# The first stage of a hybrid encoder step: weights in halves, squares behind the high halves, additions on VectorE

## The chip, the cores and the metric

The kernel runs on one core of one Trainium2 chip. Its time is device microseconds of one execution; the time of a kernel is the median of several executions. A core has five engines that work through their own queues in order and wait for one another by semaphores: TensorE (PE: matrix products; its weight loads are listed apart as PEld), VectorE (DVE), ScalarE (ACT), GpSimd (POOL) and SyncE (SP, which here issues DMAs). PE multiplies out of SBUF into PSUM, of which this kernel uses eight banks of 128 x 512 float32.

## The reference

One layer of an encoder runs over 1024 prompt rows and 128 decode rows (8 requests of 16), 1152 rows of 1024 features:

```python
h = rmsnorm(x, p['g_pre1'])
z = h @ p['w_in']                       # 1024 columns: SSM 512, pooling 256, memory queries 256
y_ssm, ... = s5_scan(u_ssm, ...)        # diagonal state space
y_pool, pool_new = multiscale_pool(u_pool, ...)
y_mem = memory_attention(q_mem, mk, mv) # mk, mv: rmsnorm(mem) @ w_mem_k, w_mem_v
gates = jax.nn.sigmoid(h @ p['w_gate'] + p['b_gate'])
merged = sum over branches of gates * (y @ w_br)
x = x + rmsnorm(merged @ p['w_out'], p['g_post1'])
x = x + rmsnorm(conv_ffn(rmsnorm(x, p['g_pre2'])), p['g_post2'])
```

with `rmsnorm(x, g) = x * rsqrt(mean(x*x) + 1e-6) * g`. Only the first normalisation, the first columns of `z`, and the normalisation and products of the 256 memory tokens are touched here.

## The kernel before, in words

Activations lie transposed: features on the 128 partitions in 8 slices (k), the rows in three chunks of 384 columns. Each float32 operand of a product is split in two: a high part, rounded to TensorE's fast format, and a low part, the rest. For a weight, `split` has ACT write `whi` (L63) and DVE `wlo` (L64). For the activations, `feat_split` has ACT write `hhi` (L126, times the gain) and DVE `hlo` (L127), slice by slice. `mm3` then makes three products for each slice (L103 hhi by whi, L106 hlo by whi, L107 hhi by wlo), so a tile of 128 output columns by one chunk (`z_tile`) is 24 products of 128x384.

The factor rsqrt(mean) is not applied before the product. While PE multiplies the unscaled rows, the sums of squares are made beside it: `feat_sq` squares a chunk in four pieces of two slices (L140 on ACT, or L142 on POOL), adds them in pairs (L144, on POOL), and adds the two rests on DVE (L148, L149). `feat_cols` has PE sum over the partitions (L156, three small products, one for each block of 128 rows, into the bank `ss`). `rsqrt` is ACT's `rs_v` (L84) and POOL's power -0.5, `rs_y` (L86). `row_bcast` has ACT write three diagonal matrices (L94 `diag`), which PE multiplies by ones (L96), so that the factor of each row stands in all partitions; ACT copies it to `rb` (L177). Then `done` scales the finished tile (`scaled`, DVE L200, `sg`) and sends it to DRAM in pieces (L883).

`start` does this for the first three blocks of `w_in` (two, called the pair, and the third, `w2`) over the three chunks, and then makes the memory tokens' keys and values (`mem_load`, `mem_split`, `mem_kv`, `mem_out`). The finished tiles lie in PSUM until `rb` of their chunk is there. PSUM has two tags of four banks: "c" (`pc`) and "s" (`ps`); a fifth `pc` tile waits until `done` has read the first one. The SSM's parameters (`ssm_params`, L343 to L441, many small DVE instructions on `pr` tiles) and the first tables (L460 to L508) are put between by a scheduler.

The order on each engine comes from that scheduler: it takes instructions by priority as written, as soon as it holds them to be ready. `keep_in_program_order` (the `pin` arguments) keeps PE's products in the order of the code, `issue_after(i)` puts what follows behind instruction i on i's own engine, `high_priority` pulls ahead. Buffers: `raw` (weights as loaded) three, `w1` (split weights) six, that is three pairs; the four square tiles share the tags U (two buffers), CA and V; `sg` three.

Before the change the order in `start` is: PE makes tile 0 and 1 of chunk 0, half of tile 0 of chunk 1, then sums chunk 0's squares, then the rest of chunk 1, and so on; ACT squares chunk 0 between its high halves.

Of the kernel before, what the change touches and what calls it, by code (L numbers as in the profile page):

```python
# [32 lines left out]
class K:  # L33
# [100 lines left out]
    def feat_sq(self, P, x, n, tags, engs="AAAA", add=True):  # L134
        nc = self.nc
        sq = [P.tile([128, 2, n * 128], F32, tag=t, name="sq") for t in tags]
        for a in range(4):
            xa = x[:, 2 * a:2 * a + 2]
            if engs[a] == "A":
                nc.scalar.activation(sq[a], xa, AF.Square)  # L140
            else:
                (nc.vector if engs[a] == "V" else nc.gpsimd).tensor_mul(sq[a], xa, xa)  # L142
            if a % 2:
                nc.gpsimd.tensor_add(sq[a - 1], sq[a - 1], sq[a])  # L144
        parts = [sq[i][:, k] for i in (0, 2) for k in range(2)]
        if add:
            with self.tc.high_priority():
                nc.vector.tensor_add(sq[0], sq[0], sq[2])  # L148
                nc.vector.tensor_add(parts[0], parts[0], parts[1])  # L149
# [112 lines left out]
    def start(self, P, pair, done, z):  # L262
# [34 lines left out]
        self.h_tiles()  # L297
        self.h_split(x2, lo)
        self.h_rows(P, rms(0, 3), 0, True)
        with self.tc.issue_after(self.diag.ins):  # L300
            self.h_split(x2, up)
# [13 lines left out]
        with self.tc.issue_after(self.diag.ins):
            w2 = self.load_w(I["w_in"][2])
            q2 = self.feat_sq(P, x2, 3, tags, "AAAA")
# [9 lines left out]
            xm = self.mem_load()  # L327
            wk = [self.load_w(I["w_mk"][h], sh) for h in range(2)]
            self.feat_sums(P, xm, 2, ss[:, 9:11], tags, "AAAA")
            mem = self.mem_split(xm)  # L330
            rsm = self.mem_rows(P, rms(9, 2))
            self.mem_out(P, "mk", self.mem_kv(mem, "mk", wk), *rsm)
# [1511 lines left out]
```

## Time and profile before

| | us |
|---|---|
| median of the runs (3) | 1606.23 |
| lowest, highest | 1605.18, 1611.32 |
| the profiled execution | 1607.13 |
| its span | 1605.3 |
| PE busy in the span | 1546.5 (96%) |
| weight loads busy | 1512.9 (94%) |
| DVE busy | 1044.1 (65%) |
| ACT busy | 586.4 (37%) |
| POOL busy | 510.8 (32%) |

A profile is one execution. Each of its rows has a source line, an engine, an operation, and the tiles as "out<-in"; L126 is line 126 of the kernel before. An engine is busy when it computes, not when it waits or issues DMAs. The time behind "idle" is how long the engine stood before an instruction, and the name behind the arrow is what ended that: the instruction that came last of those it waited for. A wait matters to the end only where PE stands still for it, since PE is busy nearly all the time. A busy PE can still be slow: the granted clock says which share of its full clock TensorE had.

### The profile page before, as it was taken

Reading aid. Unit: us, or ns where it says so; the run is one execution under the profiler, and the core shown is the slowest. Engines: PE = TensorE matmul, PEld = TensorE weight load, DVE = VectorE, ACT = ScalarE, POOL = GpSimd, SP = SyncE. Lnnn points to the kernel's source line nnn. Section 1 sums busy time; section 2 is a strip of 40 time slices with the busy share of each in tenths; the row PEclk is TensorE's granted clock in tenths of the full one; section 3 lists DMA queues with packets and bytes.
Section 4 is the critical chain, followed back from the end, with each engine's and each line's share of the span. In section 5 each row is a group of like instructions: output and inputs, shape, how many; then the busy total and the mean of one; then the engine's idle time right before and its main releaser. Section 6 shows DMA issues by size and latency. Waiting matters only on the chain.

```text
span 1605.3 us, 22914 instructions
## 1 busy us (share of the span) xinstructions
PE 1546.5 (96%) x8964; PEld 1512.9 (94%) x8964; DVE 1044.1 (65%) x1602; ACT 586.4 (37%) x894; POOL 510.8 (32%) x460
## 2 busy tenths in 40 slices
PE   6899999999999999999889999999999999999996
PEld 5899999789899999999879999999999998999996
DVE  7873997655743354637777565656565658788866
ACT  6322544442421242435435433333333333333321
POOL 2400001100021143300016435443443326655546
PEclk9899999999999999999789999999999999999998
DMA  6343333434332235122323211221212143133214
GB/s 247 98 150 96 101 110 107 162 106 117 105 120 81 67 84 164 54 91 91 114 89 138 82 69 66 72 82 69 76 62 82 70 136 137 48 101 105 89 65 167
DMA packets 98460, 163.44 MB, mean 102 GB/s; under 512 B 23216, under 2 KB 68656, under 8 KB 98352
## 3 DMA queue, kind: packets, MB, share of 16 engines
q1 hardware_dynamic: 97920, 161.75, 30.5%
q8 instruction: 70, 1.15, 0.3%
q14 instruction: 38, 0.31, 0.1%
q10 hardware_dynamic: 432, 0.23, 0.0%
HBM read 119.52 MB, written 42.42 MB: 101 GB/s over the span
## 4 chain that ended last, share of the span: by engine, by line
PE 80%; DVE 9%; DMA 3%; issue 2%; ACT 2%; POOL 1%; POOLq 0%; SPq 0%; DVEq 0%; ACTq 0%
PE pc L107 15%; PE pc L103 15%; PE pc L106 14%; PE ps L103 11%; PE ps L106 11%; PE ps L107 11%; DMA Ts<-DG 1%; PE ps L849 1%; DMA DG<-gs 1%; DVE wlo L64 1%; DVE Xs L598 1%; PE ps L1072 1%; DVE mg L1124 1%; PE ps L763 0%; DVE sg L200 0%
## 5 line engine op out<-in xcount | busy, mean ns | idle before, releaser
L103 PE MATMUL pc<-hhi,whi 128*128 128x384 f32 x760 | 259.1, 341 | 7.3 <-ACT hhi L126 7.3
L106 PE MATMUL pc<-hlo,whi 128*128 128x384 f32 x760 | 258.4, 340 | 2.7 <-DVE hlo L127 2.7
L107 PE MATMUL pc<-hhi,wlo 128*128 128x384 f32 x760 | 257.9, 340 | 0.3 <-DVE wlo L64 0.3
L63 ACT ACTIVATE whi<-rawt 128x1024 fp32r<-128x1024 f32 x102 | 107.5, 1055 | 188.6 <-PE pc L106 83.4
L64 DVE TENSOR_TENSOR wlo<-rawt,whi 128x1024 fp32r<-128x1024 f32 x102 | 128.5, 1262 | 56.2 <-ACT whi L63 55.8
L103 PEld LDWEIGHTS pc<-hhi,whi 128*128 128x128 f32 x760 | 144.6, 190 | 9.8 <-ACT hhi L126 7.3
L106 PEld LDWEIGHTS pc<-hlo,whi 128*128 128x128 f32 x760 | 144.2, 190 | 5.4 <-DVE hlo L127 3.6
L107 PEld LDWEIGHTS pc<-hhi,wlo 128*128 128x128 f32 x760 | 144.3, 190 | 2.3 <-issue 0.7
L200 DVE TENSOR_TENSOR sg<-pc,rb 128x384 f32<-128x384 f32 x95 | 52.3, 553 | 117.8 <-PE pc L107 117.4
L107 PE MATMUL pc<-h2hi,wlo 128*128 128x384 f32 x352 | 119.1, 338 | 2.1 <-DVE wlo L64 2.0
L103 PE MATMUL pc<-h2hi,whi 128*128 128x384 f32 x352 | 118.3, 336 | 0.0
L106 PE MATMUL pc<-h2lo,whi 128*128 128x384 f32 x352 | 118.2, 336 | 0.0
L63 ACT ACTIVATE S<-S 128x512 fp32r<-128x512 f32 x88 | 55.3, 630 | 157.9 <-PE ps L107 89.8
L64 DVE TENSOR_TENSOR S<-S,S 128x512 fp32r<-128x512 f32 x88 | 72.5, 826 | 56.2 <-ACT S L63 54.2
L924 ACT ACTIVATE sg<-sg,vec 128x384 f32<-128x384 f32 x72 | 44.1, 613 | 139.0 <-DVE sg L200 108.3
L1011 POOL TENSOR_TENSOR mg<-mg,sgl 128x384 f32<-128x384 f32 x24 | 29.1, 1212 | 165.4 <-DVE sgl L1009 162.0
L103 PE MATMUL ps<-bT,S 128*128 128x384 f32 x240 | 80.2, 334 | 0.0
L107 PE MATMUL ps<-bT,S 128*128 128x384 f32 x240 | 80.2, 334 | 0.0
L106 PE MATMUL ps<-bT,S 128*128 128x384 f32 x240 | 80.2, 334 | 0.0
L63 ACT ACTIVATE dhi<-dwr 128x1024 fp32r<-128x1024 f32 x38 | 39.7, 1058 | 95.2 <-PE pc L106 60.7
L107 PEld LDWEIGHTS pc<-h2hi,wlo 128*128 128x128 f32 x352 | 66.1, 188 | 2.8 <-DVE wlo L64 2.8
L1244 POOL TENSOR_TENSOR S<-rawt 128x512 f32<-128x512 f32 x20 | 27.2, 1361 | 125.6 <-PE ps L107 125.6
(463 smaller groups left out, 4349.7 us busy)
## 6 DMA issues: line engine op xcount, KB each, us to landing
rawt<-in_w_up SPq DMA_DIRECT2D x48, 512.0 KB, 3.4
Dact<-t SPq DMA_DIRECT2D x22, 576.0 KB, 3.5
rawt<-in_w_gate SPq DMA_DIRECT2D x24, 512.0 KB, 3.6
dwr<-in_w_down SPq DMA_DIRECT2D x22, 512.0 KB, 3.4
Dsg<-sg SPq DMA_DIRECT2D x45, 192.0 KB, 1.9
sgl<-Dsg SPq DMA_DIRECT2D x45, 192.0 KB, 2.4
dBr<-Dact SPq DMA_DIRECT2D x8, 768.0 KB, 5.7
xT<-in_xT SPq DMA_DIRECT2D x12, 384.0 KB, 7.6
```

The lines of the kernel that those rows point to most:

```text
L63: nc.scalar.activation(hi, src, AF.Copy)
L64: (eng or nc.vector).tensor_sub(lo, src, hi)
L103: i = nc.tensor.matmul(out, whi, xhi, start=start, stop=False)
L106: nc.tensor.matmul(out, whi, xlo, start=False, stop=False)
L107: nc.tensor.matmul(out, wlo, xhi, start=False, stop=stop)
L200: self.nc.vector.tensor_mul(sg, b, self.rb[:, c, :])
L598: V.tensor_tensor(Xs[64 * i:64 * i + 64, :, g, 1:128], m1[h, :, 0:127], m2[h, :, 0:127], op=op)
L849: nc.tensor.matmul(o, va[:, m, 2 * hp + e, :], pT[:, m, :], start=m == 0, stop=m == 1)
L924: self.nc.scalar.activation(sg, sg, AF.Sigmoid, bias=self.vec[:, V_BGATE + m:V_BGATE + m + 1])
L1011: nc.gpsimd.tensor_add(m, m, sp)
L1072: m = nc.tensor.matmul(s3[:, t:t + 1], s[:, t * 128:t * 128 + 128], self.ones[:, 0:1], start=(i, t) == (0, 0), stop=(i, t) == (len(ss) - 1 ...
L1244: G.tensor_sub(s3, a11, a21)
```

## The change

All of it is in the first stage.

- The first weight block is loaded by two DMAs of four slices each and split in two halves; chunk 0's slices 0 to 3 are split between them, slices 4 to 7 behind them.
- Squares all run on ACT. Chunk 0's stand behind the high halves of chunk 1 (`issue_after(a.ins)`), chunk 1's behind those of chunk 2.
- The additions in pairs (L144) go from POOL to DVE.
- PE sums chunk 0's squares behind both whole tiles of chunk 1, and not between the halves of the first. The row broadcast of chunk 0 stands in the middle of tile 0 of chunk 2, the sums of chunk 1 behind that tile.
- The memory tokens are split like the activations, slice by slice with the gain in the instruction (ACT L126, DVE L127, `mhi`, `mlo`); before, POOL multiplied by the gain (L224) and made the low part (L64).

```diff
             if a % 2:
-                nc.gpsimd.tensor_add(sq[a - 1], sq[a - 1], sq[a])
+                nc.vector.tensor_add(sq[a - 1], sq[a - 1], sq[a])
...
     def mem_split(self, x):
-        for a in range(2):
-            ks = slice(4 * a, 4 * a + 4)
-            nc.gpsimd.tensor_mul(x[:, ks], x[:, ks],
-                                 self.vec[:, V_GMEM + 4 * a:V_GMEM + 4 * a + 4, None].to_broadcast([128, 4, 256]))
-            self.split(mhi[:, ks], mlo[:, ks], x[:, ks], nc.gpsimd)
+        self.feat_split(x, mhi, mlo, V_GMEM, range(8))
...
-        rw = [self.load_raw(I["w_in"][pair[0]])]
+        halves = slice(0, 4), slice(4, 8)
+        rw = [self.rawtile([128, 8, 128])]
+        for hs in halves:
+            nc.sync.dma_start(rw[0][:, hs], I["w_in"][pair[0]][:, hs])
...
         a, v = self.h_split(x0, (0, 1))
-        w = [self.load_w(None, r=rw[0])]
+        w = [[self.w1.tile([128, 8, 128], F32R, tag="w", name=n) for n in ("whi", "wlo")]]
+        self.split(w[0][0][:, halves[0]], w[0][1][:, halves[0]], rw[0][:, halves[0]])
         lo, up = range(4), range(4, 8)
         with self.tc.issue_after(a.ins), self.tc.issue_after(v.ins):
-            self.h_split(x0, range(2, 8))
+            self.h_split(x0, (2, 3))
+            self.split(w[0][0][:, halves[1]], w[0][1][:, halves[1]], rw[0][:, halves[1]])
+            self.h_split(x0, up)
             b0 = [self.z_tile(w[0], 0, pin=True)]
             w.append(self.load_w(None, r=rw[1]))
-            q0 = self.feat_sq(P, x0, 3, tags, "AGAA")
-        self.h_tiles()
-        self.h_split(x1)
-        b0.append(self.z_tile(w[1], 0, pin=True))
-        t = self.pc()
-        self.z_tile(w[0], 1, t, lo, True)
-        self.feat_cols(q0, 3, ss[:, 0:3], True)
-        b1 = [self.z_tile(w[0], 1, t, up, True)]
-        b1.append(self.z_tile(w[1], 1, pin=True))
...
+            self.h_tiles()
+            a, _ = self.h_split(x1)
+            b0.append(self.z_tile(w[1], 0, pin=True))
+            with self.tc.issue_after(a.ins):
+                q0 = self.feat_sq(P, x0, 3, tags)
+            b1 = [self.z_tile(w[0], 1, pin=True)]
+            self.h_tiles()
+            a, _ = self.h_split(x2)
+            b1.append(self.z_tile(w[1], 1, pin=True))
+            self.feat_cols(q0, 3, ss[:, 0:3], True)
+            with self.tc.issue_after(a.ins):
+                q1 = self.feat_sq(P, x1, 3, tags)
+            t = self.sm()
+            self.z_tile(w[0], 2, t, lo, True)
+            self.h_rows(P, rms(0, 3), 0, True)
             for i in range(2):
                 done(pair[i], 0, b0[i])
-            q1 = self.feat_sq(P, x1, 3, tags, add=True)
-            t = self.sm()
-            self.z_tile(w[0], 2, t, lo, True)
+            b2 = [self.z_tile(w[0], 2, t, up, True)]
             self.feat_cols(q1, 3, ss[:, 3:6], True)
-            b2 = [self.z_tile(w[0], 2, t, up, True)]
+            q2 = self.feat_sq(P, x2, 3, tags)
```

What a scheduler makes of it is seen in the order of the instructions. First ACT, from its first split on, before the change (`rawt` is a weight as loaded, `xT` a chunk of activations, `sq` its squares; x4 means four of them in a row):

```order
L63 ACTIVATE whi<-rawt 128x1024
L126 ACTIVATE hhi<-xT,vec 128x384 x4
L140 ACTIVATE sq<-xT 128x768
L126 ACTIVATE hhi<-xT,vec 128x384 x2
L140 ACTIVATE sq<-xT 128x768
L126 ACTIVATE hhi<-xT,vec 128x384 x2
L140 ACTIVATE sq<-xT 128x768
L63 ACTIVATE whi<-rawt 128x1024
L126 ACTIVATE hhi<-xT,vec 128x384 x12
L84 ACTIVATE rs_v<-ps 128x3
```

and the same place now:

```order
L63 ACTIVATE whi<-rawt 128x512
L126 ACTIVATE hhi<-xT,vec 128x384 x4
L63 ACTIVATE whi<-rawt 128x512
L126 ACTIVATE hhi<-xT,vec 128x384 x4
L63 ACTIVATE whi<-rawt 128x1024
L126 ACTIVATE hhi<-xT,vec 128x384 x8
L140 ACTIVATE sq<-xT 128x768 x4
L126 ACTIVATE hhi<-xT,vec 128x384 x8
L140 ACTIVATE sq<-xT 128x768
L63 ACTIVATE whi<-rawt 128x1024
```

The first weight stands in two pieces, and chunk 0's squares have moved behind the high halves of chunk 1 (the x8 ahead of them).

Next DVE from the same point on, before:

```order
L64 TENSOR_TENSOR wlo<-rawt,whi 128x1024
L127 SCALAR_TENSOR_TENSOR hlo<-xT,vec,hhi 128x384 x8
L64 TENSOR_TENSOR wlo<-rawt,whi 128x1024
L127 SCALAR_TENSOR_TENSOR hlo<-xT,vec,hhi 128x384
L148 TENSOR_TENSOR sq<-sq 128x768
L127 SCALAR_TENSOR_TENSOR hlo<-xT,vec,hhi 128x384 x4
L149 TENSOR_TENSOR sq<-sq 128x384
```

and now:

```order
L64 TENSOR_TENSOR wlo<-rawt,whi 128x512
L127 SCALAR_TENSOR_TENSOR hlo<-xT,vec,hhi 128x384 x4
L64 TENSOR_TENSOR wlo<-rawt,whi 128x512
L127 SCALAR_TENSOR_TENSOR hlo<-xT,vec,hhi 128x384 x4
L64 TENSOR_TENSOR wlo<-rawt,whi 128x1024
L127 SCALAR_TENSOR_TENSOR hlo<-xT,vec,hhi 128x384 x8
L144 TENSOR_TENSOR sq<-sq 128x768 x2
L127 SCALAR_TENSOR_TENSOR hlo<-xT,vec,hhi 128x384 x2
L148 TENSOR_TENSOR sq<-sq 128x768
L127 SCALAR_TENSOR_TENSOR hlo<-xT,vec,hhi 128x384 x3
```

The pair additions L144 stand on DVE behind the low halves of chunk 1, and the last addition L149 comes two rows further down.

Last, DVE where chunk 1's squares are added, before (`pr` with a number is a parameter of the SSM):

```order
L421 RECIPROCAL pr_909<-pr_909 128x16
L200 TENSOR_TENSOR sg<-pc,rb 128x384 x2
L363 SCALAR_TENSOR_TENSOR pr_827<-pr_827,pr_849 128x16
L381 TENSOR_SCALAR pr_874<-pr_865 128x32
L382 SCALAR_TENSOR_TENSOR pr_866<-pr_865 128x32
L148 TENSOR_TENSOR sq<-sq 128x768
L363 SCALAR_TENSOR_TENSOR pr_827<-pr_827,pr_849 128x16
L383 TENSOR_SCALAR pr_874<-pr_866 128x32
L149 TENSOR_TENSOR sq<-sq 128x384
```

and now:

```order
L64 TENSOR_TENSOR wlo<-rawt,whi 128x1024
L357 TENSOR_SCALAR pr_843<-pr_841 128x16
L144 TENSOR_TENSOR sq<-sq 128x768
L358 TENSOR_SCALAR pr_843<-pr_843 128x16
L144 TENSOR_TENSOR sq<-sq 128x768
L359 SCALAR_TENSOR_TENSOR pr_844<-pr_843,pr_841 128x16
L364 TENSOR_SCALAR pr_838<-pr_843 128x16
L148 TENSOR_TENSOR sq<-sq 128x768
L360 SCALAR_TENSOR_TENSOR pr_844<-pr_843,pr_844 128x16
L365 TENSOR_SCALAR pr_838<-pr_838 128x16
L149 TENSOR_TENSOR sq<-sq 128x384
L361 TENSOR_SCALAR pr_839<-pr_844 128x16
```

The four additions stand together ahead of most of the parameters, and `done` of chunk 0 (the two L200) comes behind them.

More of the change, by code (lines that the diff above doesn't have):

```diff
@@ L217, in mem_split @@
     def mem_split(self, x):
-        nc = self.nc
         mhi = self.mtile([128, 8, 256], F32R, "mhi")
         mlo = self.mtile([128, 8, 256], F32R, "mlo")
-        for a in range(2):
-            ks = slice(4 * a, 4 * a + 4)
-            nc.gpsimd.tensor_mul(x[:, ks], x[:, ks],
-                                 self.vec[:, V_GMEM + 4 * a:V_GMEM + 4 * a + 4, None].to_broadcast([128, 4, 256]))
-            self.split(mhi[:, ks], mlo[:, ks], x[:, ks], nc.gpsimd)
+        self.feat_split(x, mhi, mlo, V_GMEM, range(8))
         return mhi, mlo
@@ L281, in start @@
         a, v = self.h_split(x0, (0, 1))
-        w = [self.load_w(None, r=rw[0])]
+        w = [[self.w1.tile([128, 8, 128], F32R, tag="w", name=n) for n in ("whi", "wlo")]]
+        self.split(w[0][0][:, halves[0]], w[0][1][:, halves[0]], rw[0][:, halves[0]])
         lo, up = range(4), range(4, 8)
         with self.tc.issue_after(a.ins), self.tc.issue_after(v.ins):
-            self.h_split(x0, range(2, 8))
+            self.h_split(x0, (2, 3))
+            self.split(w[0][0][:, halves[1]], w[0][1][:, halves[1]], rw[0][:, halves[1]])
+            self.h_split(x0, up)
             b0 = [self.z_tile(w[0], 0, pin=True)]
             w.append(self.load_w(None, r=rw[1]))
-            q0 = self.feat_sq(P, x0, 3, tags, "AGAA")
-        self.h_tiles()
-        self.h_split(x1)
-        b0.append(self.z_tile(w[1], 0, pin=True))
-        t = self.pc()
-        self.z_tile(w[0], 1, t, lo, True)
-        self.feat_cols(q0, 3, ss[:, 0:3], True)
-        b1 = [self.z_tile(w[0], 1, t, up, True)]
-        b1.append(self.z_tile(w[1], 1, pin=True))
[L297 to L301, printed above, removed]
+            self.h_tiles()
[13 more added lines that the diff above has]
+            self.h_rows(P, rms(0, 3), 0, True)
             for i in range(2):
                 done(pair[i], 0, b0[i])
-            q1 = self.feat_sq(P, x1, 3, tags, add=True)
-            t = self.sm()
-            self.z_tile(w[0], 2, t, lo, True)
+            b2 = [self.z_tile(w[0], 2, t, up, True)]
             self.feat_cols(q1, 3, ss[:, 3:6], True)
-            b2 = [self.z_tile(w[0], 2, t, up, True)]
+            q2 = self.feat_sq(P, x2, 3, tags)
             t = self.pc()
@@ L311, in start @@
             self.h_rows(P, rms(3, 3), 1, True)
+            behind = self.tc.issue_after(self.diag.ins)
             b2.append(self.z_tile(w[1], 2, t, up, True))
@@ L314, in start @@
                 done(pair[i], 1, b1[i])
-        with self.tc.issue_after(self.diag.ins):
             w2 = self.load_w(I["w_in"][2])
-            q2 = self.feat_sq(P, x2, 3, tags, "AAAA")
             done(2, 0, self.z_tile(w2, 0, pin=True))
@@ L326, in start @@
             done(2, 2, b)
[L327 to L332, printed above, removed]
+            with behind:
+                xm = self.mem_load()
+                wk = [self.load_w(I["w_mk"][h], sh) for h in range(2)]
+                self.feat_sums(P, xm, 2, ss[:, 9:11], tags, "AAAA")
+                mem = self.mem_split(xm)
+                rsm = self.mem_rows(P, rms(9, 2))
+                self.mem_out(P, "mk", self.mem_kv(mem, "mk", wk), *rsm)
             z(3)
```

## The prediction

> **What bounds the kernel now.** I read the page first (TensorE, called PE, is busy 96% of the span), then the waits of PE, then the busy time by windows of 20 us, since a share over 1605 us hides a stage. Columns: window, its length, then busy us (and instructions) of PE, weight loads, VectorE (DVE), ScalarE (ACT) and GpSimd (POOL), the granted TensorE clock, the DMA share, GB/s.
>
> ```profile
> 0.00:20.00 20.00, 10.04 (x38) 9.14 (x39) 13.33 (x16) 15.60 (x26) 6.53 (x13) 1.00 0.93 352
> 20.00:40.00 20.00, 14.84 (x85) 14.26 (x84) 18.58 (x69) 8.99 (x20) 4.91 (x3) 0.93 0.42 144
> 40.00:60.00 20.00, 15.03 (x71) 14.44 (x72) 18.15 (x49) 9.34 (x17) 8.19 (x5) 0.84 0.36 109
> 60.00:80.00 20.00, 19.70 (x100) 19.05 (x100) 17.29 (x29) 5.51 (x11) 10.61 (x6) 0.89 0.33 87
> 80.00:100.00 20.00, 20.00 (x147) 19.95 (x146) 17.81 (x58) 8.46 (x12) 3.22 (x9) 1.00 0.60 199
> 100.00:120.00 20.00, 20.00 (x117) 20.00 (x117) 10.98 (x40) 1.54 (x2) 0.25 (x2) 1.00 0.29 104
> ```
>
> PE is the bound, and from 80 us on it has no hole. In the first 60 us it idles 20.1 us, and the granted clock is below 1 in three windows. DVE is busy 85.2 us of the first 100, so it could take PE's place there; from 100 us on it has 9 us free in 20. Where PE's holes are, its timeline says (start, length, line, operation, in brackets the idle time before and what ended it):
>
> ```profile
> 7.30 0.69 PE L103 MATMUL pc<-hhi,whi 128*128 128x384 f32 x1 [7.30 <-ACT hhi L126]
> ...
> 9.86 0.69 PE L106 MATMUL pc<-hlo,whi 128*128 128x384 f32 x1 [1.87 <-DVE hlo L127]
> ...
> 11.97 0.69 PE L106 MATMUL pc<-hlo,whi 128*128 128x384 f32 x1 [0.78 <-DVE hlo L127]
> ...
> 16.62 0.40 PE L103 MATMUL pc<-hhi,whi 128*128 128x384 f32 x1
> ...
> 23.97 0.72 PE L156 MATMUL ps<-ones,sq 128*128 128x1 f32 x6
> ...
> 24.56 0.42 PE L103 MATMUL pc<-hhi,whi 128*128 128x384 f32 x1
> ...
> 38.96 1.44 PE L156 MATMUL ps<-ones,sq 128*128 128x1 f32 x6 [5.16 <-DVE sq L149]
> 40.26 0.67 PE L103 MATMUL ps<-hhi,whi 128*128 128x384 f32 x1
> ...
> 44.16 0.33 PE L103 MATMUL pc<-hhi,whi 128*128 128x384 f32 x1
> ...
> 58.29 1.44 PE L156 MATMUL ps<-ones,sq 128*128 128x1 f32 x6 [4.97 <-DVE sq L149]
> 59.59 0.67 PE L103 MATMUL pc<-hhi,whi 128*128 128x384 f32 x1
> ...
> 64.53 0.34 PE L103 MATMUL pc<-hhi,whi 128*128 128x384 f32 x1
> ...
> 70.28 0.81 PE L96 MATMUL ps<-diag,ones 128*128 128x384 f32 x2
> ```
>
> Three places: a slow start, and twice a wait for L149, the last addition of the squares of chunks 1 and 2. Behind each wait the clock is low. Fast, a product costs 0.174 us (from 64.53 to 70.28 stand 33 of them); behind the first wait 12 cost 3.90 us (40.26 to 44.16), 0.325 each, and behind the second 15 cost 4.94 us.
>
> Why L149 is late, DVE's and POOL's rows say; the last seven are groups by form (count, busy us, mean ns).
>
> ```profile
> 6.73 1.47 POOL L142 TENSOR_TENSOR sq<-xT 128x768 f32<-128x768 f32 x1 [5.09 <-DMA xT<-in_xT]
> 6.78 2.50 DVE L64 TENSOR_TENSOR wlo<-rawt,whi 128x1024 fp32r<-128x1024 f32 x1 [5.86 <-ACT whi L63]
> 9.20 7.48 DVE L127 SCALAR_TENSOR_TENSOR hlo<-xT,vec,hhi 128x384 fp32r<-128x384 f32 x8
> ...
> 19.13 2.20 DVE L127 SCALAR_TENSOR_TENSOR hlo<-xT,vec,hhi 128x384 fp32r<-128x384 f32 x4
> 30.92 3.64 POOL L144 TENSOR_TENSOR sq<-sq 128x768 f32<-128x768 f32 x2 [4.67 <-DVE pr L363]
> 31.03 1.76 DVE L371 TENSOR_TENSOR pr<-par,pr 128x16 f32<-128x16 f32 x1
> ...
> 37.32 0.95 DVE L148 TENSOR_TENSOR sq<-sq 128x768 f32<-128x768 f32 x1
> ...
> 38.36 0.55 DVE L149 TENSOR_TENSOR sq<-sq 128x384 f32<-128x384 f32 x1
> ...
> L503 DVE TENSOR_TENSOR CA<-pr,bc 128x576 f32<-128x576 f32 x1 | 2.9, 2942 | 0.0
> L506 DVE TENSOR_TENSOR CA<-pr,bc 128x576 f32<-128x576 f32 x1 | 0.7, 744 | 0.0
> L149 DVE TENSOR_TENSOR sq<-sq 128x256 f32<-128x256 f32 x1 | 2.5, 2510 | 0.0
> L148 DVE TENSOR_TENSOR sq<-sq 128x512 f32<-128x512 f32 x1 | 2.4, 2365 | 3.8 <-POOL sq L144 3.8
> L495 DVE TENSOR_TENSOR ar<-ar,tg 128x512 f32<-128x512 f32 x1 | 0.7, 683 | 0.0
> L400 DVE TENSOR_TENSOR pr<-pr 128x64 f32<-128x64 f32 x1 | 1.9, 1878 | 0.0
> L363 DVE SCALAR_TENSOR_TENSOR pr<-pr,pr 128x16 f32<-128x16 f32 x12 | 2.0, 168 | 0.1
> ```
>
> Two POOL additions run from 30.92 to 34.56, and a DVE instruction on 16 columns that starts 0.11 us after them takes 1.76 us, where L363's of that size take 0.17. Equal shapes cost 2.94 or 0.74 (L503, L506), 2.37 or 0.68 (L148, L495); eight hlo cost 0.94 each beside POOL's first additions and 0.55 alone. So POOL's long instructions hold DVE up, and both L149 stand behind such stretches on POOL and DVE.
>
> **The change, part by part.**
>
> *Start.* For the low half wlo, DVE begins at 6.78 and takes 2.50; PE starts at 7.30, waits for the first hlo until 9.86, and again 0.78.
>
> ```profile
> 5.68 1.06 ACT L63 ACTIVATE whi<-rawt 128x1024 fp32r<-128x1024 f32 x1 [3.23 <-DMA rawt<-in_w_in]
> 13.84 6.18 ACT L126 ACTIVATE hhi<-xT,vec 128x384 fp32r<-128x384 f32 x12
> 24.98 1.27 POOL L86 TENSOR_TENSOR rs_y<-rs_v,mhalf 128x3 f32<-128x3 f32 x1 [9.79 <-ACT rs_v L84]
> 26.29 0.99 ACT L94 ACTIVATE diag<-ident,rs_y 128x128 f32<-128x128 f32 x3 [1.39 <-POOL rs_y L86]
> L140 ACT ACTIVATE sq<-mem 128x512 f32<-128x512 f32 x4 | 2.5, 622 | 3.1 <-DVE sq L148 3.1
> ```
>
> Half the weight is 256 KB less to wait for: at the 352 GB/s of the first window 0.75 us, so ACT starts near 4.95 instead of 5.68. A half costs ACT 0.62 (the 128x512 row), the first hhi 0.52 (12 in 6.18), DVE 0.68 for its half of wlo, 0.55 for the first hlo: 4.95 + 0.62 + 0.68 + 0.55, with a tenth for each hand-over, gives 7.0. Nothing runs on POOL then, so a hlo comes every 0.55 us, faster than PE's three cold products (0.98). PE runs without a hole from 7.0 instead of 9.86 with a later hole of 0.78: **3.6 us**. Bounds: 2.9 if the half lands no sooner than the whole; 4.2 if the first product, which ran ahead at 7.30, counts too. The extra DMA costs SP one issue, ahead of transfers that land behind one another anyway: nothing.
>
> *Squares behind the high halves.* ACT runs 8 hhi and the next weight before chunk 0's four squares; PE's L156 of chunk 0 moves from behind 60 products to behind 96. PE: cold for some 6 us as before (9.86 to 16.62 less the hole), 18 products until 12.9, 78 at 0.174 until 26.5. Until then ACT has halves, 8 hhi, the next whi, 8 hhi (to 15.5) and 4 squares (to 18.5); DVE, with 16 hlo at 0.55 and its weights, is through at 16.9 and then adds 2 x 0.95, 0.95, 0.55 with five hlo between: L149 ends near 23.6. PE comes 2.9 us later, so this wait stays at zero.
>
> *First stall.* L149 of chunk 1 needs four squares, of which the last needs a buffer that chunk 0's L149 frees; it stands on ACT behind rs_v, which waits for L156: done near 28.3. Two additions, L148 and L149 after it on DVE: 28.3 + 0.95 + 0.95 + 0.55 = 30.8. PE reaches it after 24 products and the row broadcast, near 32.6. The stall goes with its cold tail: 5.16 + (1.30 - 0.59 for L156) + (3.90 - 12 x 0.174) = **7.7 us**. Bound: 0 to 1 us of it stays.
>
> *Second stall.* In the same way 4.97 + 0.71 + (4.94 - 15 x 0.174) = **8.0 us**: L149 of chunk 2 ends near 36.7, PE is there near 42.4.
>
> *What is late next.* L96 of chunk 0 now stands 12 products behind L156 instead of 36. From L156's end (24.56 + 0.13) to the diagonal (27.28) are 2.6 us; 12 products are 2.1. So PE waits **0.5 us**, and 0.1 at chunk 1's. Holes that short (0.78 at 11.97) did not restart the cold stretch.
>
> Rule beside row: behind waits of 5.16 and 4.97 us the cold stretches last 5.2 us (38.96 to 44.16) and 6.2 (58.29 to 64.53). [...]
>
> *DVE's load.* New on it: six additions of 128x768 (0.95), two of 128x512 (0.68), eight mlo of 128x256 (at most 0.55): at most 11.5 us. Gone with POOL's work: wlo 2.50 - 1.37, hlo 7.48 - 4.4, L371 1.76 - 0.17, L503 2.2, L149 2.0, L148 1.7, L400 at least 1.3: 13.0 from the rows shown. DVE does not grow. What POOL keeps is rs_y; its memory tokens' product and split go to ACT (eight mhi) and DVE.
>
> *Behind the stage* the order of every engine's instructions is the old one but for a few neighbours; PE has no idle time there that a shift by some us changes.
>
> Sum: 3.6 + 7.7 + 8.0 - 0.6 = 18.7 us. The profiled execution took 1607.13 us (span 1605.3), so 1588.4; the median of the runs, 1606.23, lies 0.9 lower, which gives 1587.5. I say **1588**.
>
> **The rivals.**
> - *Banks.* The second product of w_in[2] needs a PSUM bank that done(pair, 1) frees; its row evacuation rb stands on ACT behind the next whi, three squares and eight mhi. From the diagonal at 35.5: 1.06 + 3 x 0.62 + 8 x 0.52 + 0.5 gives 43.1 with L200's 0.5 to come, where PE is at 43.2. With lower costs of mhi (a third less data than hhi) it is just in time; if not, PE waits 1 to 5 us: 1589 to 1593.
> - *No gain at the start.* If the halves bring none of the 3.6 us: 1592. [...] Against it, the row above: 384 and 512 KB pieces ran the first window at a DMA share of 0.93.
> - *DVE gets behind.* 85.2 - 13.0 + 11.5 = 83.7 us of work after a start near 5.7 ends at 89.4, where PE wants to be, at what was 100.9, at 82.2. Held back by all of it, PE loses 7.2: 1595. Against it: PE has four banks, so three tiles of 24 x 0.174 us of slack, and DVE 9 us free in the window behind.
> - *Slower: DVE becomes the bound.* If its long instructions have a cause other than POOL, nothing is relieved: 85.2 + 11.5 us, every L149 and every low weight of the first 100 us comes up to 11.5 us later than before, and PE waits there: up to 1618. It decides when a 128x16 instruction takes over 1 us with POOL idle. The pairs of equal shapes speak against it.
>
> **How the numbers follow.** Forecast 0.68 (own range 1584 to 1591, from the bounds: gain 16 to 23), banks 0.10, start 0.09, DVE behind 0.08, slower 0.05. The range of 8 in 10 reaches from 1583.5 to 1596 and leaves out the slower case and tails. Half a per cent, about what a measurement tells from no change, is 8 us: faster is below 1598.2, which takes all cases but the last and a tail of DVE behind: 0.91; same 0.04; slower 0.05.
>
> **What would show it.** In the changed profile: PE from near 7.0 with no hole over 0.3 us until L96; L156 of chunk 0 near 26.5; no wait for L149; a wait of about 0.5 us for diag; L96 of chunk 2 near 51.6 instead of 70.28; no DVE instruction of 16 columns over 1 us; clock 1.00 in every window behind the first. Wrong it would be if PE waited over 2 us for L149, L200 or whi before 60 us, or if the 18.7 us were there at 70 us and gone at 160.

## The result, and the profile after

The changed kernel took 1586.47 us (median of 4 runs, 1585.59 to 1588.48), the kernel before 1607.98 on the same chip (4 runs): a ratio of 0.9873, with a 95% interval from 0.9855 to 0.9891. The forecast of 1588, in its range of 1583.5 to 1596, held. The profiled execution took 1587.11 us with a span of 1585.3, which is 20.0 less than the span before.

One execution of one experiment (before_dve) ran at a granted clock of 0.68; it is left out of that ratio, and its rows come from a second run of the same kernel, before_dve2.

First PE's waits in the first 200 us of the changed kernel (total us, times, longest):

```profile
PE pc L103 <- ACT hhi L126: 6.6, 1, 6.6
PE ps L96 <- ACT diag L94: 1.2, 1, 1.2
PE pc L107 <- DVE wlo L64: 0.7, 2, 0.4
```

The two waits for L149 (10.1 us) and those for hlo (2.7) have gone. What is left of the first stage's waits after the start is 1.2 for the diagonal and 0.7 for low weights (0.39 at 13.81, 0.29 at 54.37). The windows of 20 us, columns as before:

```profile
0.00:20.00 20.00, 12.96 (x62) 11.74 (x63) 12.62 (x23) 15.04 (x26) 1.08 (x10) 1.00 0.93 339
20.00:40.00 20.00, 18.80 (x107) 17.63 (x107) 18.86 (x46) 18.09 (x38) 2.07 (x2) 1.00 0.58 190
40.00:60.00 20.00, 19.71 (x114) 19.05 (x114) 19.26 (x104) 8.37 (x18) 2.08 (x2) 1.00 0.51 143
```

In the first 60 us PE is busy 51.5 us where it was 39.9, the clock is 1.00 in all three, and GpSimd (POOL) has 5.2 us of work where it had 19.6. The places in PE's timeline on which the sum rested:

```profile
6.59 0.69 PE L103 MATMUL pc<-hhi,whi 128*128 128x384 f32 x1 [6.59 <-ACT hhi L126]
7.34 0.69 PE L106 MATMUL pc<-hlo,whi 128*128 128x384 f32 x1
...
10.07 0.35 PE L103 MATMUL pc<-hhi,whi 128*128 128x384 f32 x1
...
26.07 0.72 PE L156 MATMUL ps<-ones,sq 128*128 128x1 f32 x6
...
30.19 0.91 PE L96 MATMUL ps<-diag,ones 128*128 128x384 f32 x2 [1.18 <-ACT diag L94]
...
33.02 0.72 PE L156 MATMUL ps<-ones,sq 128*128 128x1 f32 x6
...
42.96 0.72 PE L156 MATMUL ps<-ones,sq 128*128 128x1 f32 x6
...
51.97 0.81 PE L96 MATMUL ps<-diag,ones 128*128 128x384 f32 x2
```

The last of these, the row scale of chunk 2, is the mark by which all kernels below are compared: it stood at 70.28, so the first stage gained 18.3 us. The rows of VectorE (DVE) that PE waited for, or could have:

```profile
23.99 0.55 DVE L149 TENSOR_TENSOR sq<-sq 128x384 f32<-128x384 f32 x1
...
30.73 0.55 DVE L149 TENSOR_TENSOR sq<-sq 128x384 f32<-128x384 f32 x1
...
36.70 0.56 DVE L149 TENSOR_TENSOR sq<-sq 128x384 f32<-128x384 f32 x1
...
39.59 0.17 DVE L371 TENSOR_TENSOR pr<-par,pr 128x16 f32<-128x16 f32 x1
...
42.66 1.01 DVE L200 TENSOR_TENSOR sg<-pc,rb 128x384 f32<-128x384 f32 x2
```

Each L149 now ends 1.5 to 5.7 us ahead of the L156 that reads it, and L371, 1.76 us before, takes 0.17.

### The profile page after: what moved, and what is told of

It is laid out like the page before. It is cut to its first block, busy times and chain, and to the rows that moved or that the text cites. A ratio compares the mean times of both kernels' runs of the same rounds, so it can differ in the third digit from the quotient of the medians.

```text
span 1585.3 us, 22927 instructions
## 1 busy us (share of the span) xinstructions
PE 1539.2 (97%) x8964; PEld 1506.2 (95%) x8964; DVE 1035.0 (65%) x1619; ACT 589.0 (37%) x902; POOL 487.1 (31%) x447
## 4 chain that ended last, share of the span: by engine, by line
PE 81%; DVE 9%; DMA 3%; ACT 3%; issue 2%; POOL 1%; SPq 0%; POOLq 0%; DVEq 0%; ACTq 0%
PE pc L107 15%; PE pc L103 15%; PE pc L106 15%; PE ps L103 11%; PE ps L106 11%; PE ps L107 11%; DVE dB L64 1%; DMA Ts<-DG 1%; PE ps L849 1%; DMA DG<-gs 1%; ACT hhi L126 1%; DMA dwr<-in_w_down 1%; PE ps L1072 1%; DVE mg L1124 1%; DVE wlo L64 0%
## 5 line engine op out<-in xcount | busy, mean ns | idle before, releaser
L63 ACT ACTIVATE whi<-rawt 128x1024 fp32r<-128x1024 f32 (+1 forms) x103 | 107.7, 1046 | 187.0 <-PE pc L106 86.5
L64 DVE TENSOR_TENSOR wlo<-rawt,whi 128x1024 fp32r<-128x1024 f32 (+1 forms) x103 | 127.4, 1239 | 56.3 <-ACT whi L63 55.8
L200 DVE TENSOR_TENSOR sg<-pc,rb 128x384 f32<-128x384 f32 x95 | 52.3, 554 | 117.3 <-PE pc L107 116.1
L63 ACT ACTIVATE S<-S 128x512 fp32r<-128x512 f32 x88 | 55.2, 630 | 158.5 <-PE ps L107 89.8
L64 DVE TENSOR_TENSOR S<-S,S 128x512 fp32r<-128x512 f32 x88 | 72.5, 826 | 56.2 <-ACT S L63 54.2
L103 PE MATMUL pc<-mhi,whi 128*128 128x384 f32 x192 | 66.8, 348 | 0.0
```

What stands on the lines that cost most here:

```text
L63: nc.scalar.activation(hi, src, AF.Copy)
L64: (eng or nc.vector).tensor_sub(lo, src, hi)
L103: i = nc.tensor.matmul(out, whi, xhi, start=start, stop=False)
L200: self.nc.vector.tensor_mul(sg, b, self.rb[:, c, :])
```

## The experiments

The theory: GpSimd's instructions on tensors hold VectorE's, VectorE's last additions come late, and PE waits for them and then works at about half rate for some us (0.325 us a product for 0.174). The change pays because it takes the additions and the memory keys' split off GpSimd *and* puts the sums where VectorE is through. Its rivals: the order alone is the gain, or the engine alone.

"On the changed kernel" is worked out from the ratios: the changed kernel measured 0.9873 on one chip and 0.9880 (0.9861 to 0.9899) on another; the difference to each, times 1606 us, gives the two ends. By the intervals each is uncertain by 3 to 5 us, so that of the rows below after_again only the first four differ surely from the changed kernel; of the others the marks say more. Only d6_set and best ran on the same chip as after_again. A second thing limits the comparison: the scheduler sorts the instructions anew for each kernel. VectorE's order is the changed kernel's, but for a few instructions, in the first 60 us of d6_add, d6_set and whole_w; in the other variants of the changed kernel it differs in many places. The mark is the row scale of chunk 2 in that kernel's profile.

| kernel | ratio to the kernel before (95%) | on the changed kernel, us | mark, us |
|---|---|---|---|
| changed kernel, again (after_again) | 0.9880 (0.9861 to 0.9899) | | 51.67 |
| additions on GpSimd again (add_pool) | 0.9962 (0.9949 to 0.9974) | +13 to +14 | 65.07 |
| memory split on GpSimd again (mem_pool) | 0.9939 (0.9925 to 0.9952) | +9 to +11 | 51.57 |
| GpSimd work for nobody (d6_add) | 0.9920 (0.9895 to 0.9945) | +6 to +8 | 56.33 |
| sums early again (sums_early) | 0.9919 (0.9893 to 0.9945) | +6 to +7 | 56.88 |
| weight whole again (whole_w) | 0.9899 (0.9884 to 0.9914) | +3 to +4 | 52.77 |
| squares first again (sq_first) | 0.9898 (0.9870 to 0.9925) | +3 to +4 | 53.88 |
| constants on GpSimd (d6_set) | 0.9881 (0.9866 to 0.9897) | 0 to +1 | 52.52 |
| row scale later (late_rows) | 0.9877 (0.9853 to 0.9901) | -1 to +1 | 50.11 |
| the same, first high half first (best) | 0.9880 (0.9863 to 0.9897) | 0 to +1 | 50.98 |
| kernel before, additions on VectorE (before_dve; the mark is before_dve2's) | 0.9995 (0.9986 to 1.0004) | | 63.53 |

**add_pool**: the changed kernel without its first line.

```diff
             if a % 2:
-                nc.vector.tensor_add(sq[a - 1], sq[a - 1], sq[a])
+                nc.gpsimd.tensor_add(sq[a - 1], sq[a - 1], sq[a])
```

> The changed kernel, with the two additions at L144 of every feat_sq back on GpSimd; all else stays. The theory of the prediction (GpSimd's work holds VectorE's instructions, and so the last addition, L149, comes late): VectorE slips 3 to 6 us between 10 and 45 us of the profile, L149 of chunk 1 comes near 32 us where TensorE wants it at 33, and the first tile of chunk 2's second product waits 2 to 3 us for a bank; +2 to +4 us on the changed kernel, 1588.5 to 1590.5. The rival that the engine of the additions is the whole matter: both stalls come back, +8 to +16 us. The rival that the order is the whole matter: within 1 us of the changed kernel.

Measured: +13 to +14, far over the theory's +2 to +4 and inside the range of its rival. PE's waits in its first 200 us:

```profile
PE pc L103 <- DVE sg L200: 5.0, 1, 5.0
PE ps L96 <- ACT diag L94: 3.3, 2, 2.0
PE ps L156 <- DVE sq L149: 1.3, 2, 0.7
```

The order keeps most of the two old stalls away (1.3 us in the place of 10.1), so the engine is not the whole matter for these two waits. What comes instead is the bank that the prediction's first rival named: 5.0 us for L200. How that comes about, the rows of DVE say:

```profile
30.79 1.79 DVE L361 TENSOR_SCALAR pr<-pr 128x16 f32<-128x16 f32 x1
...
36.48 0.55 DVE L149 TENSOR_TENSOR sq<-sq 128x384 f32<-128x384 f32 x1
...
47.79 2.29 DVE L127 SCALAR_TENSOR_TENSOR mlo<-mem,vec,mhi 128x256 fp32r<-128x256 f32 x3
...
53.48 1.01 DVE L200 TENSOR_TENSOR sg<-pc,rb 128x384 f32<-128x384 f32 x2
```

L149 of chunk 1 comes 5.8 us later than in the changed kernel, three mlo cost 2.29 where they cost 1.27, and L200 starts at 53.48 where it started at 42.66. I had priced one slip of 3 to 6 us, and it is 11 by then. Added up, the low halves, parameters and mlo that ran beside GpSimd's work before this L200 took some 9.5 us more than their undisturbed lengths. VectorE's order differs too: 52 small parameter instructions stand ahead of this L200 that stand behind it in the changed kernel; at their spacing there they take some 6 us, about as much as the seven additions that are no longer VectorE's. No run separates the two. Of the 3.3 us for the diagonal, a wait of 2.05 at 31.84 had a cold stretch behind it, too (products 0.32 us apart until 35.66).

**before_dve and before_dve2**: the kernel before with only that line changed.

```diff
-                nc.gpsimd.tensor_add(sq[a - 1], sq[a - 1], sq[a])
+                nc.vector.tensor_add(sq[a - 1], sq[a - 1], sq[a])
```

> The kernel before, with only the additions at L144 on VectorE. The theory of the prediction: the sums of squares come 4 to 6 us earlier, so that the wait of L156 for the squares (10.1 us in the kernel before) falls to 2 to 5; the start and GpSimd's work on the memory keys stay; 8 to 12 us under the kernel before, near 1598. The rival that the order is the whole matter: within 2 us of the kernel before. The rival that the engine is the whole matter: 14 to 17 us under it.

Measured: no change (0.9986 to 1.0004; before_dve2's one run took 1607.40 us). The theory's 8 to 12 us are not there, and the rival that the order is everything looks right. The second run was to show whether the order holds the sums:

> The same kernel as before_dve, for a profile at the full clock. The theory that the order holds the sums in the kernel before, so that the engine of the additions is nothing there: TensorE waits for the sum of chunk 1 (L156) about as long as before, L149 of chunk 1 at 37 to 39 us of the profile, behind the products with the row scale (L200) that wait for chunk 0's; its third row scale (L96) within 2 us of the kernel before's 70.28. The rival that the gain in the first stage is real and is lost later: the third row scale 5 us or more earlier.

The third row scale came 6.75 us earlier, so the rival holds: the order alone does not keep the gain away. PE's timeline in that run:

```profile
34.82 0.83 PE L156 MATMUL ps<-ones,sq 128*128 128x1 f32 x6 [2.51 <-DVE sq L149]
...
51.62 1.44 PE L156 MATMUL ps<-ones,sq 128*128 128x1 f32 x6 [4.79 <-DVE sq L149]
...
63.53 0.81 PE L96 MATMUL ps<-diag,ones 128*128 128x384 f32 x2
...
68.69 0.69 PE L107 MATMUL pc<-hhi,wlo 128*128 128x384 f32 x1 [3.05 <-DVE wlo L64]
...
77.84 0.59 PE L96 MATMUL ps<-diag,ones 128*128 128x256 f32 x2
```

The sums of chunk 0 stand at 22.49 where they stood at 23.97, the first wait fell from 5.16 to 2.51, and behind it PE did not turn cold (products 0.17 us apart from 35.77 on). The order has its share in what is left of that wait: L149 of chunk 1 stands at 34.21, behind the two L200 of chunk 0, which start at 32.25. But the second wait stays (4.79), and 5 us behind the mark stands a new wait of 3.05 for a low weight, with a cold stretch after it. By the row scale of the memory keys (the last row; 79.91 in the kernel before) only 2.1 us are left. GpSimd and VectorE there, first GpSimd's rows, then VectorE's:

```profile
54.64 1.89 POOL L224 TENSOR_TENSOR mem<-mem,vec 128x1024 f32<-128x1024 f32 x1
56.49 5.19 POOL L64 TENSOR_TENSOR mlo<-mem,mhi 128x1024 fp32r<-128x1024 f32 x2
```

```profile
54.70 2.38 DVE L148 TENSOR_TENSOR sq<-sq 128x512 f32<-128x512 f32 x1
57.00 2.38 DVE L613 TENSOR_TENSOR sd<-pr,h 128x32 f32<-128x32 f32 x1
59.30 2.67 DVE L149 TENSOR_TENSOR sq<-sq 128x256 f32<-128x256 f32 x1
...
67.42 1.22 DVE L64 TENSOR_TENSOR wlo<-rawt,whi 128x1024 fp32r<-128x1024 f32 x1
```

Three VectorE instructions take 7.4 us while GpSimd works on the memory keys; the sum of them alone would be some 1.3 (0.68, 0.18 and 0.41 in their undisturbed rows). The low weight stands behind them. So the gain was real and was given back some us later to the same cause in another place. Where the last 1 to 2 us went isn't settled: two executions of one kernel differ by as much (after_again, below).

**mem_pool**: the changed kernel with the old split of the memory keys.

```diff
-        self.feat_split(x, mhi, mlo, V_GMEM, range(8))
+        for a in range(2):
+            ks = slice(4 * a, 4 * a + 4)
+            nc.gpsimd.tensor_mul(x[:, ks], x[:, ks],
+                                 self.vec[:, V_GMEM + 4 * a:V_GMEM + 4 * a + 4, None].to_broadcast([128, 4, 256]))
+            self.split(mhi[:, ks], mlo[:, ks], x[:, ks], nc.gpsimd)
```

> The changed kernel, with the memory keys' split back in the form of the kernel before (products and subtractions on GpSimd). The theory that GpSimd's work holds VectorE's: 9 us of GpSimd work lies beside VectorE's busy stretch from 28 us of the profile on, where a bank comes free about 1 us before TensorE wants it; +2 to +5 us. The rival that GpSimd's work hurts VectorE only through the sums that wait for it: within 0.5 us.

Measured: +9 to +11, over both. Its mark is the changed kernel's (51.57), so all of it stands behind. PE's timeline, then two rows of VectorE:

```profile
54.77 0.44 PE L103 MATMUL pc<-hhi,whi 128*128 128x384 f32 x1 [1.45 <-DVE sg L200]
...
60.39 0.69 PE L107 MATMUL pc<-hhi,wlo 128*128 128x384 f32 x1 [4.99 <-DVE wlo L64]
...
71.04 0.59 PE L96 MATMUL ps<-diag,ones 128*128 128x256 f32 x2
```

```profile
46.52 2.37 DVE L368 SCALAR_TENSOR_TENSOR pr<-pr,pr 128x16 f32<-128x16 f32 x1
...
59.12 1.21 DVE L64 TENSOR_TENSOR wlo<-rawt,whi 128x1024 fp32r<-128x1024 f32 x1
```

The wait for the low weight that ate the gain of before_dve2 is here again (4.99, and 1.45 for L200), and the memory's row scale stands 10.8 us behind the changed kernel's 60.22. Four instructions on 16 or 32 columns, at 38.66, 44.79, 46.52 and 51.38, ran beside GpSimd's work and took 1.71 to 2.37 us each in place of 0.17, some 7.5 us together, and the low weight behind them came 6.0 us later than in the changed kernel (59.12 for 53.09). VectorE's order differs here as well, and the run doesn't separate that. Taken back alone, the memory keys' split costs half of what the whole change gains; the prediction didn't price it on its own.

**d6_add and d6_set**: GpSimd's work without anyone who needs it. Twelve instructions meant to stand beside the low halves of chunks 1 and 2, in d6_add each adding a high half to itself, in d6_set (with `nc.gpsimd.memset(scr, 1.0)` in the place of the last two lines of `dummy`) writing a constant. Nobody reads `scr`. d6_set was to tell apart two cases: any work of GpSimd holds VectorE, and eight low halves of chunk 1 take over 6 us beside the constants (+2 to +5 us); or only work that reads operands does, and they take 4.3 us as in the changed kernel (within 1 us of it).

```diff
+        scr = P.tile([128, 384], F32, tag="scr", name="scr")
+
+        def dummy():
+            for k in range(6):
+                h = self.hhi[-1][:, k].bitcast(F32)
+                nc.gpsimd.tensor_add(scr, h, h)
...
             a, _ = self.h_split(x1)
+            dummy()
...
             a, _ = self.h_split(x2)
+            dummy()
```

> The changed kernel plus twelve additions on GpSimd (128x384 each) that read the high halves of chunks 1 and 2 and write a tile that nobody reads: GpSimd's work without anyone waiting for its result. The theory that GpSimd's work holds VectorE's instructions: VectorE between 13 and 27 us of the profile shows instructions of 1 to 2.5 us in the place of 0.6, it falls 4 to 9 us behind, L149 of chunk 1 and the low halves of chunk 2 come late, and TensorE waits; +3 to +8 us. The rival that GpSimd's work costs only through those who wait for it or stand behind it on its queue: within 1 us (a delay of rs_y behind it by up to 1 us counts to this).

Measured: +6 to +8, and 4.4 to 4.7 at the mark, as the theory has it. The additions ran from 12.35 to 26.6 us. VectorE's rows in d6_add:

```profile
12.94 8.89 DVE L127 SCALAR_TENSOR_TENSOR hlo<-xT,vec,hhi 128x384 fp32r<-128x384 f32 x8
21.75 3.08 DVE L144 TENSOR_TENSOR sq<-sq 128x768 f32<-128x768 f32 x2
24.75 2.28 DVE L127 SCALAR_TENSOR_TENSOR hlo<-xT,vec,hhi 128x384 fp32r<-128x384 f32 x2
...
27.82 1.67 DVE L127 SCALAR_TENSOR_TENSOR hlo<-xT,vec,hhi 128x384 fp32r<-128x384 f32 x3
29.48 0.55 DVE L149 TENSOR_TENSOR sq<-sq 128x384 f32<-128x384 f32 x1
```

and the same eight low halves in the changed kernel:

```profile
13.68 4.32 DVE L127 SCALAR_TENSOR_TENSOR hlo<-xT,vec,hhi 128x384 fp32r<-128x384 f32 x8
```

Nobody waits for the twelve additions, VectorE's order here is the changed kernel's, and eight low halves cost 8.89 us in the place of 4.32; as soon as GpSimd is done, three cost 1.67 again. ScalarE was not held: its eight high halves beside the same additions took 4.15 us in both kernels. L149 comes 5.5 us late and PE waits 3.51 for it. This is the run that separates being held from waiting for a result. The low halves took 1.11 us each for 0.54; by what means the one engine holds the other, no run shows. An instruction with one tensor operand was slow as well: L356 took 1.77 us at 32.82 in the kernel before, beside two additions of GpSimd (30.92 to 34.56), and 0.17 in the changed kernel (26.13).

> The changed kernel plus twelve writes of a constant on GpSimd (128x384 each, no operand read) in the places of the twelve additions of d6_add. [...]

Measured: 0 to +1 and no wait for VectorE's sums. But this run tells less than it was meant to: the constants depend on nothing, so GpSimd wrote them between 1.5 and 7.2 us, ahead of the low halves of chunk 1. Beside them stood three VectorE instructions only, a half wlo of 0.69 us and two hlo of 1.14 together, and none was longer than in the changed kernel (0.69 and 1.14). That GpSimd must read to hold VectorE is suggested, not shown.

**sums_early**: the column sums of chunk 0 between the halves of chunk 1's first tile, as before.

```diff
-            b1 = [self.z_tile(w[0], 1, pin=True)]
+            t = self.pc()
+            self.z_tile(w[0], 1, t, lo, True)
+            self.feat_cols(q0, 3, ss[:, 0:3], True)
+            b1 = [self.z_tile(w[0], 1, t, up, True)]
...
-            self.feat_cols(q0, 3, ss[:, 0:3], True)
```

> The changed kernel, with the column sums of chunk 0 (L156) moved up again between the two halves of the first tile of chunk 1, where the kernel before has them. The theory that TensorE's sums must come behind VectorE's last addition: TensorE reaches them near 19.5 us of the profile, L149 ends at 24.5, so that it waits 4 to 5 us, works at a lower clock for some us behind that, and saves the wait of 1.2 us for diag; +4 to +7 us on the changed kernel. The rival that their place is nothing, because chunk 1's products wait for something else anyway: within 1 us.

Measured: +6 to +7, and 4.9 to 5.2 at the mark. The row in PE's timeline, and the first product that is 0.34 us long again:

```profile
24.09 0.87 PE L156 MATMUL ps<-ones,sq 128*128 128x1 f32 x6 [4.56 <-DVE sq L149]
...
28.15 0.34 PE L106 MATMUL pc<-hlo,whi 128*128 128x384 f32 x1
```

A wait of 4.56 and ten slow products. So the place of the sums is worth as much as the theory said. In the kernel before, where the squares stand between the high halves, the same place cost no wait at chunk 0 (L156 at 23.97): the two moves belong together.

**sq_first**: chunk 0's squares asked for ahead of chunk 1's high halves.

```diff
+            q0 = self.feat_sq(P, x0, 3, tags)
             self.h_tiles()
             a, _ = self.h_split(x1)
             b0.append(self.z_tile(w[1], 0, pin=True))
-            with self.tc.issue_after(a.ins):
-                q0 = self.feat_sq(P, x0, 3, tags)
```

> The changed kernel, with chunk 0's four squares ahead of chunk 1's high halves on ScalarE, and not behind them. Theory: the high halves come 3 us later (the first at 15.4 us of the profile in place of 12.4, the last at 19.6 in place of 16.5), TensorE wants the first of them near 17.7 and one each 0.52 us from there, so they stay ahead of it by a little, but VectorE's low halves follow 1 us behind and the additions come ahead of them: waits for hlo of 0 to 2 us; 0 to +2 us on the changed kernel. The rival that this place is what makes the change pay: +5 us or more.

Measured: +3 to +4, between the two. The squares went further forward than meant, between chunk 0's own last high halves; PE's first tile then had holes of 0.36 and 0.33 us, and it was cold until 15.97 us, where the changed kernel was until 10.07. The waits are small; most of the 2 us at the mark is that cold stretch, which the holes seem to lengthen (last section).

**whole_w**: the first weight in one transfer and one split.

```diff
-        for hs in halves:
-            nc.sync.dma_start(rw[0][:, hs], I["w_in"][pair[0]][:, hs])
+        nc.sync.dma_start(rw[0], I["w_in"][pair[0]])
...
-        self.split(w[0][0][:, halves[0]], w[0][1][:, halves[0]], rw[0][:, halves[0]])
+        self.split(w[0][0], w[0][1], rw[0])
```

> The changed kernel, with the first weight in one transfer and one split. If the halves bring the gain at the start: the first product starts at 8.0 to 8.5 us of the profile instead of 6.59, +1.4 us, and up to 3.6 us if the low half (wlo) is late too. The rival that they bring nothing (the transfer of the first half lands no sooner than the whole would): within 0.5 us of the changed kernel.

Measured: +3 to +4, of which 0.8 to 1.1 stand at the mark. PE's start, and VectorE's first row:

```profile
7.35 0.69 PE L103 MATMUL pc<-hhi,whi 128*128 128x384 f32 x1 [7.35 <-ACT hhi L126]
8.63 0.69 PE L106 MATMUL pc<-hlo,whi 128*128 128x384 f32 x1 [0.59 <-DVE hlo L127]
```

```profile
6.82 1.23 DVE L64 TENSOR_TENSOR wlo<-rawt,whi 128x1024 fp32r<-128x1024 f32 x1 [5.91 <-ACT whi L63]
```

The second product comes 1.3 us later, as expected. In the kernel before it came 1.2 us later still, at 9.86, and the whole low weight cost 2.50 beside GpSimd's square and costs 1.23 here. So about half of these 2.5 us belongs to the halves, and half, by VectorE's row, to the square that left GpSimd (no run puts that square back alone). At chunk 0's L156 the halves are worth 1.9 us (27.95 for 26.07). Of the rest of the +3 to +4, 2.1 us stand far behind: three waits for sums between 690 and 806 us of the program, which stand two lines higher in this kernel (L1070), come to 12.8 us where the changed kernel's (L1072) come to 10.7. VectorE's order differs there by a few instructions; whether that is the cause was not tested.

**late_rows and best**: the row scale of chunk 0 behind 21 products and not 12; in best also the first high half ahead of the weight's split.

```diff
-            self.z_tile(w[0], 2, t, lo, True)
+            self.z_tile(w[0], 2, t, range(7), True)
...
-            b2 = [self.z_tile(w[0], 2, t, up, True)]
+            b2 = [self.z_tile(w[0], 2, t, range(7, 8), True)]
```

> The changed kernel, with the row scale of chunk 0 (diag, L96) behind 21 products of the tile of chunk 2 and not behind 12. TensorE comes to it 1.6 us later, so that its wait of 1.18 us for diag goes; -1.2 us on the changed kernel if nothing else is late. The rival: the row scale's copy (rb, L177) and the products with it on VectorE (L200) come 0.4 us later, no bank comes free later than TensorE wants it, so the wait is all there is; -0.5 to -1.2. If L200 is late for a bank: +0.5.

Measured: the wait is gone and the mark stands at 50.11, 1.6 to 1.9 us earlier. The time doesn't show it (-1 to +1, with an interval of 0.9853 to 0.9901): this size can't be told from nothing here.

> The changed kernel, with the row scale of chunk 0 behind 21 products as in late_rows, and with the first high half of chunk 0 (hhi, L126) ahead of the first weight's split on ScalarE. In the changed kernel ScalarE waits till 5.40 us for the weight and splits it before it makes the high half that the first product waits for. If the states and the scales have landed by 4.9 us, the first product starts near 6.05 in place of 6.59: -0.5 us, and with the wait for diag -1.5 to -2 us on the changed kernel. The rival: they land later than the weight, and only the wait for diag goes, -1.2; or what comes behind the first stage takes the gain back, 0.

Measured: no gain on the changed kernel. ScalarE (ACT) in best, and PE's first product:

```profile
4.71 1.28 ACT L126 ACT_TABLE_LOAD   x1 [4.71 <-DMA xT<-in_xT]
6.01 0.61 ACT L126 ACTIVATE hhi<-xT,vec 128x384 fp32r<-128x384 f32 x1
```

```profile
7.20 0.69 PE L103 MATMUL pc<-hhi,whi 128*128 128x384 f32 x1 [7.20 <-ACT whi L63]
```

The states had landed at 4.71, as hoped. But the table load, which the changed kernel does at 1.18 us while it waits for the weight, now waits for the states itself, and its 1.28 us stand on the path. The first product came 0.6 us later, not 0.5 earlier.

**after_again**: the changed kernel, run once more.

> The changed kernel once more, unchanged, as the measure for the kernels on the same chip. If the 1.7 us by which it gained more than its first stage (18.3 of 20.0 us between the two profiles) are chance between two executions: the span behind the first stage, from the third row scale (L96, 51.97 us) to the end, differs by about 1 us between this profile and the one shown, and the gain on the kernel before is 18 to 20 us. If they belong to the change: the same span to 0.3 us.

Measured: a span of 1583.0 us for the same program, 2.3 less than in the profile above, of which 0.3 stand at the mark. One row of attention (32 of its products, first and last start), in the profile above and here:

```profile
L849 PE MATMUL ps<-at x32: 591/592/676, 318.6 to 400.7; 128*128 128x512 f32 x32
```

```profile
L849 PE MATMUL ps<-at x32: 591/592/676, 318.4 to 398.9; 128*128 128x512 f32 x32
```

1.6 us of the difference arise between these two ends. So 1.7 us of gain outside the first stage are no more than two executions of one kernel differ by: from the mark on the two differ by 2.0.

## Why the prediction was right

**Start** (3.6 us forecast). Before, 60 products were done at 23.97; 36 more at 0.174 would have ended at 30.2, and the changed kernel has its 96 done at 26.07: 4.2 us. Parts of the step were off and in part cancelled, which is luck. ACT began with the half weight at 5.40, not 4.95, since the half landed later than its bytes at the window's rate say; so the second product came at 7.34 and not 7.0. PE had a hole of 0.39 for a low weight at 13.81, over the 0.3 that the prediction allowed as its sign. The cold stretch lasted 3.5 us (6.59 to 10.07), not 6; in after_again it lasted 5.1, so this length is chance. And whole_w gives only half of the gain to the halves. A sentence of the prediction seems wrong besides: that holes like the one of 0.78 at 11.97 do not restart the cold stretch. The runs speak for it that they do (last section), so the start without holes could also be cold for a shorter time, which the step had left at its old length. For a hole at full rate the sentence came out right: behind the 1.18 at 30.19 the products are 0.17 us apart again from 31.11 on. The first product's start hardly differs from what it was (6.59 for 7.30); the holes behind it were the cost.

**L156 of chunk 0 and both stalls** (15.7 us). L156 stood at 26.07 (26.5 forecast) with L149 at 23.99 to 24.54 (23.6); for chunk 1 L149 ended at 31.28 (30.8) and PE came at 33.02 (32.6); for chunk 2 at 37.26 (36.7) and 42.96 (42.4). Mechanism and size held.

**What is late next** (0.6 us): 1.2. The step counted rs_v right behind L156, but ACT did something else first:

```profile
26.59 0.96 ACT L607 ACTIVATE Xs<-h 64x32 f32<-64x32 f32 x4
27.58 0.17 ACT L84 ACTIVATE rs_v<-ps 128x3 f32<-128x3 f32 x1
```

L156 ended at 26.79, and rs_v started 0.8 us later behind the four copies of the scan's state. They stand ahead of it in ACT's order, and the step left them out. At chunk 1 PE lost 0.2 (35.96 where the spacing of the products gives 35.77), for 0.1 forecast.

**VectorE's load** does not grow. It is busy 85.2 us of the first 100 before and after, but PE is 18 us further by then, so these are not the same work; over the first 120 it is 89.8 for 96.1. The forecast 83.7 can't be read off directly. No instruction on 16 columns took over 1 us. The pairs of equal shapes were the right evidence: d6_add shows the cause that they suggested. The slower rival fell with it, and with L371's 0.17.

**The rivals.** VectorE did not get behind. Banks did not bind, but nearly: the first of the two L200 was through near 43.2 us (half of 1.01 from 42.66), some 0.4 before PE's next tile, and add_pool, where it is 11 us later, shows the 5 us which that rival had priced at 1 to 5.

**The sum**: 18.7 forecast, 18.3 at the mark (4.2 + 15.7 - 1.2 is 18.7; the other 0.4 are the 0.2 at chunk 1 and 0.1 for each of the two broadcasts that now stand inside a tile). That the start gave 0.6 more and the diagonal 0.6 less than forecast, so that the sum stayed, is luck. The other 1.7 of the 20.0 between the spans are chance, as after_again has it.

What I had not seen is how the parts hang together. Undone one at a time, additions, memory split and sums cost 13, 10 and 6 us, squares and halves 3 each (these two within the noise); the first three alone come to more than the whole change brings, and the first of them done alone in the kernel before brings nothing. A stage that runs with 0.4 to 1.7 us to spare at most of its hand-overs can lose a wait and a cold stretch to any one of them.

## What to carry to other kernels

Ask of each instruction that GpSimd runs beside VectorE not who waits for its result, but what VectorE does meanwhile (eight low halves took 8.89 us in d6_add and 4.32 without the additions): two instructions of equal shape and different length in one trace are the sign (2.94 and 0.74 us for L503 and L506 in the kernel before). When a move gains at one mark and not at the end, follow the marks one after the other; here the gain of before_dve2 went 5 us behind the place where it had been made. And test a change of several parts both ways, one part alone and all but one: the two answers here, nothing and 13 us, are both right.

## What the runs showed of the hardware

The cold stretch (products 0.32 us apart, where they are 0.17 apart later) is not one figure, and holes in it seem to restart it. From PE's first product to the first at full rate it took, in the profiles whose PE had no hole over 0.1 us in it (but for some 0.27 behind the first product: the second came 0.75 us after it, 0.48 in best), 3.4 us (mem_pool), 3.5 (the changed kernel), 4.1 (late_rows, d6_add), 4.7 (sums_early), 5.1 (after_again), 5.4 (add_pool) and 5.6 (best). In those with holes of 0.25 (in d6_set, by the spacing of the products) to 1.9 us it took 6.1 (before_dve2), 7.2 (whole_w), 7.4 (d6_set) and 9.6 (sq_first; the kernel before too, by the first product of 0.34 us, at 16.85). Counted from the start of the product behind the last hole, these five took 3.6, 5.9, 4.0, 3.6 and 4.9, as long as the others. The same program took 3.5 and 5.1. The profiles without holes spread over 2.2 us, and what sets the length was not shown. In the kernel before, the cold stretches behind the two waits for L149 took 5.2 and 6.2 us, at a granted clock of 0.51 and 0.50 (38.96 to 44.16, 58.29 to 64.53); at the start of the changed kernel (6.59 to 10.07), with products as far apart, the profile gives a clock of 1.00. At 0.32 against 0.174 us a product, 2 us of the cold stretch are worth about 0.9. No run tried a hole by itself, so this is a pattern over thirteen executions, not a test. Once PE was at full rate, not every wait made it cold. In the first stage of these kernels the products stayed 0.17 us apart behind waits of 0.25 to 1.22 us (1.18 for the diagonal in the changed kernel); behind one of 1.45 (mem_pool) only two products stand. They were 0.32 apart behind all eight waits of 3.05 to 5.16 and behind one of 2.05 (add_pool), but not behind one of 2.51 (before_dve2).

GpSimd's twelve additions, 14.1 us of its work, cost VectorE 6.9 us (8.89, 3.08 and 2.28 against 4.32, 1.92 and 1.14). The first ACT table load went, in the changed kernel and in best, with the instruction that ACT had first. In the changed kernel that is the weight's split, and the load took its 1.28 us from 1.18 on, while the weight was still under way. In best it is the first high half, and the load began only when the states had landed (4.71).
